# A work list that knows VectorE's and GpSimd's common port, v summed by VectorE alone, one-hots of build on TensorE

## The chip, the cores and the metric

The kernel runs on one core of one Trainium2 chip. TensorE (PE) multiplies matrices and loads weights (PEld), VectorE (DVE), ScalarE (ACT) and GpSimd (POOL) work element by element, SyncE (SP) issues plain DMAs, and GpSimd also issues the indirect DMAs that gather rows by index. The metric is the time of one execution in microseconds (us); lower is better. Of the kernel before there are three timed runs: 3367.77, 3373.03 and 3373.15 us, median 3373.03.

## The reference

Two transformer blocks follow each other on one sequence of 256 tokens of width 2048, in float32. The change lies in the last part, the PEER layer (product keys, `peer_sublayer`) of the second block. For each of two blocks of 128 tokens, 8 heads and 16 choices a head:

```
q = (hb @ w_query).reshape(PEER_BLOCK, PEER_HEADS, 2, D_KEY // 2)
s = jnp.einsum('thpc,hpnc->thpn', q, sub_keys).astype(jnp.float32)
top_s, top_i = lax.top_k(s, PEER_TOPK)
cand_s = (top_s[:, :, 0, :, None] + top_s[:, :, 1, None, :]).reshape(PEER_BLOCK, PEER_HEADS, -1)
cand_i = (top_i[:, :, 0, :, None] * N_KEYS + top_i[:, :, 1, None, :]).reshape(PEER_BLOCK, PEER_HEADS, -1)
best_s, best_j = lax.top_k(cand_s, PEER_TOPK)
idx = jnp.take_along_axis(cand_i, best_j, axis=-1)
g = jax.nn.softmax(best_s, axis=-1)
u_sel = jnp.take(u, idx, axis=0)
a = jax.nn.gelu(jnp.einsum('thkd,td->thk', u_sel, hb), approximate=False)
v_sel = jnp.take(v, idx, axis=0)
return jnp.einsum('thk,thkd->td', (g * a).astype(hb.dtype), v_sel)
```

`u` and `v` have 16384 rows (128 x 128 pairs of half keys) of 2048 columns each. A token picks 8 x 16 = 128 experts, so both blocks together have 256 gathers of 128 rows, one row for each token of a block.

## The kernel before

Everything up to the PEER layer is scheduled by the framework. The PEER layer is ordered by `Plan`, a list of operations with their estimated costs, run once while the program is built: each engine has a clock, an operation is ready when what it comes after is done, and the engine that can start first takes the ready operation with the lowest key. `plan.choice` offers an operation to two engines, and the clocks choose. The order that comes out is the order of each engine's instructions; on the chip nothing of the costs is left, only waits for data and for buffers. A `ring` stands for the buffers of one tile.

The stages, in the order of time:

- **Query and routing** (`plan_query`, `plan_route`): 32 tiles of `w_query` are split into a high and a low part (`hi` on ACT, `lo` on DVE or POOL), multiplied with the tokens, and 16 units (head and block) pick their 16 best keys on DVE. POOL multiplies the one-hot places `eq` with the keys' numbers (L1568).
- **Scores** (`plan_scores`, `plan_gather_u`): the upper 1024 columns of all u rows are multiplied densely on PE in 128 tiles e, into S. The lower 1024 columns are gathered for the chosen rows only, and multiplied with the tokens by DVE (L1680) or by POOL and ACT (L1686, L1687).
- **Pick** (`plan_pick`): the chosen scores are taken out of S. For 4 tokens at once PE forms a distance between key numbers from their digits (`far`, L1789), ACT makes a one-hot matrix of it with Relu (`near`, L1793), PE multiplies (L1798), DVE selects (L1804). `plan_coef` then makes the weights `cf` of a block: gelu times softmax.
- **Build** (`plan_weights`): S is filled again, now with the weights of all 16384 experts for each token. For 4 tokens DVE makes two one-hot matrices by comparing an iota with the key numbers, `ohb` (L1858) and `oha` (L1864, four instructions, times the weight), PE multiplies them (L1870), ACT moves the product to S (L1874). Block 0 of build overlaps block 1 of pick.
- **Out** (`plan_out`, `plan_gather_v`): columns 768 to 2047 of v are multiplied densely on PE in 128 tiles e: load `vraw`, `vhi` on ACT (L1953), `vlo` on DVE (L1957), the weights' halves `wh` on ACT and `wl` on DVE (L1965), and three products (hi hi, lo hi, hi lo) in that order (L1970). Columns 0 to 767 are gathered for the chosen rows (L1902) and summed: DVE multiplies and adds in one instruction into `vacc0` (L1909), or ACT scales (L1916) and POOL adds into `vacc1` (L1921); at the end the two are merged (L2007).

An indirect DMA stands in POOL's own instruction stream, so POOL's sums and the gathers queue behind each other. SP issues all loads in order.

## Time and profile before

| what | value |
|---|---|
| median of three runs | 3373.03 us |
| profiled execution | 3370.8 us, span 3369.1 us |
| PE busy, share of span | 2915.7 us, 87% |
| VectorE busy | 2602.2 us, 77% |
| GpSimd busy | 1492.3 us, 44% |
| DMA, mean over the span | 224 GB/s |

The span runs from the first to the last instruction; 1.7 us lie around it. The PEER layer's own stages begin at about 1754 us. A window's row gives each engine's busy time in it, then the granted clock of TensorE (1.0 is 2.4 GHz, 0.5 is 1.2 GHz), the DMA engines' busy share, and GB/s. Busy time of an instruction includes time in which it has been started and is held up.

### The profile page before, as it was taken

How to read it: one execution, taken by the hardware profiler on the slowest of the kernel's cores; microseconds unless marked ns; L12 is line 12 of the kernel's file. 1: busy time of each engine (PE TensorE's matmuls, PEld its weight loads, DVE VectorE, ACT ScalarE, POOL GpSimd, SP SyncE). 2: the span in 40 equal slices, each digit the busy share in tenths (PEclk: the TensorE clock that was granted, in tenths of full speed). 3: DMA queues.
4: the chain of work that ended last, by engine and by line, in shares of the span. 5: the costliest groups of instructions: out<-in, count | busy, mean ns of one | idle time of the engine just before them, and what ended most of it. 6: DMA issues, size and time to landing. Idle time of an engine off the chain costs nothing.

```text
span 3369.1 us, 45653 instructions
## 1 busy us (share of the span) xinstructions
PE 2915.7 (87%) x16134; PEld 2456.3 (73%) x16134; DVE 2602.2 (77%) x4256; ACT 1646.7 (49%) x2629; POOL 1492.3 (44%) x994
## 2 busy tenths in 40 slices
PE   3598899799999999999988889998977767888887
PEld 1475677677888778988768788888865655777775
DVE  7879877868656655555558998888867998999898
ACT  5555545545444544544544444444434455555554
POOL 3324433402000000000005666788867757988887
PEclk9699998899999999999989899999977878999999
DMA  8777876756655555544565378999965337888887
GB/s 298 231 253 250 280 244 216 257 164 221 181 157 162 175 157 144 151 132 137 156 223 185 118 225 299 342 340 338 348 201 174 112 89 246 288 308 292 303 297 248
DMA packets 293393, 753.05 MB, mean 224 GB/s; under 512 B 32430, under 2 KB 39524, under 8 KB 292780
## 3 DMA queue, kind: packets, MB, share of 16 engines
q1 hardware_dynamic: 235216, 513.03, 48.0%
q0 software_dynamic: 57344, 234.91, 20.0%
q8 instruction: 127, 2.08, 0.3%
q10 hardware_dynamic: 604, 2.19, 0.2%
q14 instruction: 102, 0.84, 0.1%
HBM read 743.48 MB, written 6.55 MB: 223 GB/s over the span
## 4 chain that ended last, share of the span: by engine, by line
PE 38%; DVE 20%; DMA 12%; POOL 12%; issue 10%; ACT 3%; POOLq 0%; DVEq 0%; SPq 0%; ACTq 0%
PE b_mm L387 7%; PE b_mm L386 7%; PE b_mm L388 7%; DMA mraw<-in_w_mod 6%; PE b_mm L1970 4%; DMA gathered<-in_peer_u,idx 3%; POOL gathered L1686 3%; POOL vacc L1921 3%; POOL gathered L1674 3%; DVE vlo L1957 2%; POOL gathered L1902 2%; PE b_mm L408 2%; PE b_mm L406 2%; PE b_mm L407 2%; DVE lo L361 2%
## 5 line engine op out<-in xcount | busy, mean ns | idle before, releaser
L361 DVE TENSOR_TENSOR lo<-raw,hi 128x1024 fp32r<-128x1024 f32 (+2 forms) x456 | 571.6, 1255 | 351.9 <-ACT hi L360 349.9
L360 ACT CAST hi<-raw 128x1024 fp32r<-128x1024 f32 (+2 forms) x456 | 464.6, 1021 | 453.6 <-PE b_mm L388 275.9
L387 PE MATMUL b_mm<-lo,hh 128*128 128x512 f32 (+1 forms) x1536 | 620.0, 404 | 30.0 <-DVE lo L361 26.8
L388 PE MATMUL b_mm<-hi,hl 128*128 128x512 f32 (+1 forms) x1536 | 604.3, 398 | 0.5 <-DVE hl L638 0.5
L386 PE MATMUL b_mm<-hi,hh 128*128 128x512 f32 (+1 forms) x1536 | 581.7, 402 | 9.3 <-ACT hi L360 7.1
L1902 POOL DMA_INDIRECT gathered<-in_peer_v,idx x256 | 333.7, 1303 | 99.6 <-issue 31.2
L387 PEld LDWEIGHTS b_mm<-lo,hh 128*128 128x128 f32 x1536 | 295.3, 192 | 109.7 <-DVE lo L361 49.6
L1674 POOL DMA_INDIRECT gathered<-in_peer_u,idx x256 | 296.0, 1156 | 163.0 <-DVE gathered L1680 53.9
L554 POOL TENSOR_TENSOR macc<-macc,mraw 128x512 f32<-128x512 f32 x112 | 179.6, 1604 | 420.8 <-ACT mraw L552 386.0
L386 PEld LDWEIGHTS b_mm<-hi,hh 128*128 128x128 f32 x1536 | 293.3, 192 | 84.2 <-ACT hi L360 11.5
L388 PEld LDWEIGHTS b_mm<-hi,hl 128*128 128x128 f32 x1536 | 293.9, 192 | 62.7 <-DVE hl L638 1.0
L1680 DVE SCALAR_TENSOR_TENSOR gathered<-gathered,hn 128x1024 f32<-128x1024 f32 x159 | 284.3, 1802 | 65.7 <-DMA gathered<-in_peer_u,idx 65.5
L1741 PE MATMUL b_mm<-hd,ulo 128*128 128x256 f32 x1024 | 301.8, 295 | 27.3 <-DVE ulo L1731 26.5
L1739 PE MATMUL b_mm<-hd,uhi 128*128 128x256 f32 x1024 | 308.6, 301 | 10.4 <-ACT uhi L1727 10.0
L1921 POOL TENSOR_TENSOR vacc<-vacc,gathered 128x768 f32<-128x768 f32 x154 | 302.0, 1961 | 33.4 <-ACT gathered L1916 30.4
L1740 PE MATMUL b_mm<-hd,uhi 128*128 128x256 f32 x1024 | 294.2, 287 | 0.0
L1957 DVE TENSOR_TENSOR vlo<-vraw,vhi 128x1280 fp32r<-128x1280 f32 x128 | 268.2, 2096 | 3.9 <-ACT vhi L1953 3.7
L1686 POOL TENSOR_TENSOR gathered<-gathered,hn 128x1024 f32<-128x1024 f32 x97 | 235.7, 2430 | 24.5 <-DMA gathered<-in_peer_u,idx 19.7
L1741 PEld LDWEIGHTS b_mm<-hd,ulo 128*128 128x128 f32 x1024 | 200.5, 196 | 40.9 <-DVE ulo L1731 40.5
L1970 PE MATMUL b_mm<-vlo,wh 128*128 128x512 f32 x512 | 166.2, 417 | 65.7 <-DVE vlo L1957 65.6
L1739 PEld LDWEIGHTS b_mm<-hd,uhi 128*128 128x128 f32 x1024 | 201.0, 196 | 14.4 <-ACT uhi L1727 14.3
L1740 PEld LDWEIGHTS b_mm<-hd,uhi 128*128 128x128 f32 x1024 | 201.2, 196 | 0.0
(616 smaller groups left out, 6493.5 us busy)
## 6 DMA issues: line engine op xcount, KB each, us to landing
raw<-in_w_in SPq DMA_DIRECT2D x336, 512.0 KB
mraw<-in_w_mod SPq DMA_DIRECT2D x192, 512.0 KB
vraw<-in_peer_v SPq DMA_DIRECT2D x128, 640.0 KB
uraw<-in_peer_u SPq DMA_DIRECT2D x123, 512.0 KB
raw<-in_w_out SPq DMA_DIRECT2D x96, 512.0 KB
raw<-in_peer_w_query SPq DMA_DIRECT2D x32, 512.0 KB
raw<-in_w_in SPq DMA_DIRECT2D x16, 256.0 KB
gathered<-in_peer_u,idx POOLq DMA_INDIRECT x256, 7.2
```

Source lines behind the costliest of these rows:

```text
L360: nc.scalar.copy(hi[:, :, :n], raw[:, :, :n])
L361: nc.vector.tensor_tensor(lo[:, :, :n], raw[:, :, :n], hi.bitcast(F32)[:, :, :n], ALU.subtract)
L386: nc.tensor.matmul(o, ah[:, kk, s], hi[:, k, :n], start=kk == 0, stop=False)
L387: nc.tensor.matmul(o, ah[:, kk, s], lo[:, k, :n], start=False, stop=False)
L388: nc.tensor.matmul(o, al[:, kk, s], hi[:, k, :n], start=False, stop=kk == KT - 1)
L1674: nc.gpsimd.indirect_dma_start(out=g, out_offset=None, in_=rows, in_offset=bass.IndirectOffsetOnAxis(ap=self.idx[h, t][:, k:k + 1], axis=0))
L1686: nc.gpsimd.tensor_tensor(s["g"], s["g"], self.hn[:, t, :], ALU.mult)
L1739: nc.tensor.matmul(o, h["hi"][:, k, :], hh[:, kk, :], start=kk == 0, stop=False)
L1740: nc.tensor.matmul(o, h["hi"][:, k, :], hl[:, kk, :], start=False, stop=False)
L1741: nc.tensor.matmul(o, h["lo"][:, k, :], hh[:, kk, :], start=False, stop=kk == UD - 1)
L1902: nc.gpsimd.indirect_dma_start(out=g, out_offset=None, in_=rows, in_offset=bass.IndirectOffsetOnAxis(ap=self.idx[h, t][:, k:k + 1], axis=0))
L1921: plan.op("POOL", 2.05, lambda o: nc.gpsimd.tensor_tensor(a, a, s["g"], ALU.add), key - 12, after=[o], frees=[(gv, s["op"]), (poolq, o)], ...
```

## The change

- `Plan` gets a clock `shared`. An operation that is marked (`two`, or `True` behind its cost) starts in the list only when the previous marked one is over, on whichever engine. Marked are DVE operations of several kinds and POOL's product of gathered u rows. Several costs are new numbers.
- The low halves of `w_query` (1024 columns) that stood on POOL, 11 of the 32, and the 16 products of `eq` with the keys' numbers (512 columns) go from POOL to DVE.
- Every sum of gathered v rows is done by DVE into one `vacc`; ACT's scaling, POOL's adding, `vacc1` and the merge are gone.
- `GV` goes from 768 to 736, so PE's dense part of v is 1312 columns wide. There are 4 gather buffers of v at first, not 3. In the list, gathers from number 90 on come after the load of a tile e that rises with the number ("tied to tiles"). On the chip this is no wait: it sets places in the engines' order.
- Build's one-hots come from digits, as pick's do: PE forms distances for both key numbers (`far`: 8 matmuls of 128 columns on 32 rows), DVE compares the one in PSUM with zero distance and multiplies with the weight in a single instruction (`ohb`), and ACT makes the other with Relu (`oha`). For this the digits of both key numbers are split, stored and loaded again; squares and casts of them go to ACT. Pick's and build's distances use the `mm` banks, build's products the `tr` banks.

```diff
-GV = 768
+GV = 736
+RX = 4
+EARLY = 90
...
     def start(self, o, a):
-        t = max(self.clock[a[0]], o.ready)
+        t = max(self.clock[a[0]], o.ready, self.shared if a[5] else 0.0)
...
             end = self.clock[e] = t + cost
+            if two:
+                self.shared = end
...
-                c = plan.choice([("DVE", 1.28, lambda o, f=lo: f(o, nc.vector), (), 0),
-                                 ("POOL", 2.5, lambda o, f=lo: f(o, nc.gpsimd), (), 0)], key - 80, after=[b],
-                                takes=[r[2]], frees=[(r[0], a)])
+                c = plan.op("DVE", 1.26, lo, key - 80, after=[b], takes=[r[2]], frees=[(r[0], a)], two=True)
...
-        def marked(o):
+        def negated(o):
             nm = s["nm"] = sp.tile([P, 1], F32, name="nm", tag="nm", bufs=2)
             nc.gpsimd.tensor_scalar(nm, s["best"][:, 0:1], -1.0, None, op0=ALU.mult)
-            nc.gpsimd.tensor_tensor(s["eq"], s["eq"], s["indf"][:, :, None, :].to_broadcast(FOUR), ALU.mult)
...
         def numbers(o):
+            nc.vector.tensor_tensor(s["eq"], s["eq"], s["indf"][:, :, None, :].to_broadcast(FOUR), ALU.mult)
...
-                plan.choice([("DVE", 1.42, dot, (), 0), ("POOL", 2.5, product, (poolq,), 0)], key, after=[o])
+                plan.choice([("DVE", 1.31, dot, (), 0, True), ("POOL", 2.45, product, (poolq,), 0, True)], key,
+                            after=[o])
...
+            def far(o, n=n, s=s):
+                r1, r, c = self.distance(t, n)
+                s["p1"], s["p2"] = self.bank("mm", 4), self.bank("mm", 4)
+                for i in range(4):
+                    nc.tensor.matmul(s["p1"][:, i * P:(i + 1) * P], r1[:, i * P:(i + 1) * P], c, start=True, stop=True)
+                for i in range(4):
+                    nc.tensor.matmul(s["p2"][:, i * P:(i + 1) * P], r[:, i * P:(i + 1) * P], c, start=True, stop=True)
+
+            def first(o, n=n, s=s):
                 s["b"] = self.vp.tile([P, 4, P], F32, name="ohb", tag="ohb", bufs=3)
-                nc.vector.tensor_tensor(s["b"], self.iota[:, None, :].to_broadcast([P, 4, P]),
-                                        self.byexp[t][:, 1, n:n + 4, None].to_broadcast([P, 4, P]), ALU.is_equal)
-
-            def first(o, n=n, s=s):
-                s["a"] = a = self.vp.tile([P, 4, P], F32, name="oha", tag="oha", bufs=4)
+                nc.vector.scalar_tensor_tensor(s["b"], s["p1"].rearrange("p (a b) -> p a b", a=4), 1.0,
+                                               self.byexp[t][:, 2, n:n + 4, None].to_broadcast([P, 4, P]),
+                                               op0=ALU.is_equal, op1=ALU.mult)
+
+            def second(o, s=s):
+                s["a"] = self.vp.tile([P, 4, P], F32, name="oha", tag="oha", bufs=3)
+                nc.scalar.activation(s["a"], s["p2"].rearrange("p (a b) -> p a b", a=4), AF.Relu)
...
-                        nc.scalar.activation(a if fresh else s["g"], s["g"], AF.Identity, scale=c)
...
-                            plan.op("POOL", 2.05, lambda o: nc.gpsimd.tensor_tensor(a, a, s["g"], ALU.add), key - 12,
...
+                    o = plan.op("POOL", 1.08, gather, key - 25, after=[*last, *pace], takes=[gv], kb=GV / 2)
                     last = [o.issued]
-                    plan.choice([("DVE", 1.06, add, (), 0), ("ACT", 0.98, scale, (poolq,), 0)], key,
-                                after=[o, self.cf_done[t][1]])
+                    plan.op("DVE", 0.12 + GV * 1.16e-3, add, key, after=[o, self.cf_done[t][1]], frees=[(gv, o)],
+                            signals=[self.added], two=True)
```

Where the list places things, at three places. **VectorE in build**, where blocks 1 of pick (`pjunk`) and 0 of build meet. Before:

```order
L1804 SCALAR_TENSOR_TENSOR pjunk,dots_22902<-iota_22905,byexp_22904,b_at 128x128 x4
L1858 TENSOR_TENSOR ohb<-iota_22905,byexp_22903 128x512
L1864 TENSOR_SCALAR oha<-iota_22905,byexp_22903 128x128 x4
L1858 TENSOR_TENSOR ohb<-iota_22905,byexp_22903 128x512
L1804 SCALAR_TENSOR_TENSOR pjunk,dots_22902<-iota_22905,byexp_22904,b_at 128x128 x4
L1864 TENSOR_SCALAR oha<-iota_22905,byexp_22903 128x128 x4
```

Now, at the same place:

```order
L1932 SCALAR_TENSOR_TENSOR vacc<-gathered,cf_23638,vacc 128x736
L1815 SCALAR_TENSOR_TENSOR pjunk,dots_22905<-iota_22908,byexp_22907,b_at 128x128 x4
L1877 SCALAR_TENSOR_TENSOR ohb<-b_mm,byexp_22906 128x512
L1932 SCALAR_TENSOR_TENSOR vacc<-gathered,cf_23638,vacc 128x736 x2
L1815 SCALAR_TENSOR_TENSOR pjunk,dots_22905<-iota_22908,byexp_22907,b_at 128x128 x4
L1877 SCALAR_TENSOR_TENSOR ohb<-b_mm,byexp_22906 128x512
```

The five comparisons of a tile on VectorE have become one, and sums of gathered v rows (L1932) stand between. In the order before, 7 sums stand on VectorE ahead of the first `wl` of out; now 83 do, 26 of them ahead of block 1's weights.

**VectorE in out**, in the middle of the tiles. Before:

```order
L1965 TENSOR_TENSOR wl<-S,wh 128x256
L1909 SCALAR_TENSOR_TENSOR vacc_22892<-gathered,cf_24598,vacc_22892 128x768
L1957 TENSOR_TENSOR vlo<-vraw,vhi 128x1280
L1965 TENSOR_TENSOR wl<-S,wh 128x256
L1957 TENSOR_TENSOR vlo<-vraw,vhi 128x1280
```

Now:

```order
L1975 TENSOR_TENSOR wl<-S,wh 128x256
L1932 SCALAR_TENSOR_TENSOR vacc<-gathered,cf_24776,vacc 128x736
L1967 TENSOR_TENSOR vlo<-vraw,vhi 128x1312
L1932 SCALAR_TENSOR_TENSOR vacc<-gathered,cf_24776,vacc 128x736
L1975 TENSOR_TENSOR wl<-S,wh 128x256
L1967 TENSOR_TENSOR vlo<-vraw,vhi 128x1312
```

A tile has one or two sums on VectorE; 88 of the 256 stand ahead of the first `vlo`, 179 ahead of the 65th, and the last one stands ahead of the 123rd.

**GpSimd in out.** Before:

```order
L1902 DMA gathered<-in_peer_v,idx 128x768 x2
L1921 TENSOR_TENSOR vacc_22893<-vacc_22893,gathered 128x768
L1902 DMA gathered<-in_peer_v,idx 128x768 x2
L1921 TENSOR_TENSOR vacc_22893<-vacc_22893,gathered 128x768
L1902 DMA gathered<-in_peer_v,idx 128x768
```

Now, from the last product of u rows to the end:

```order
L1684 DMA gathered<-in_peer_u,idx 128x1024 x3
L1696 TENSOR_TENSOR gathered<-gathered,hn 128x1024
L1925 DMA gathered<-in_peer_v,idx 128x736 x252
L2050 UNCONDITIONAL_BRANCH
```

No sum is left on GpSimd behind the u rows. Of the 256 gathers of u, 214 stood ahead of pick's first instruction on GpSimd (an iota) and 42 behind it; now 208 and 48.

## Rows read from the trace of the kernel before

**Rows 1.** Busy time by stage: routing and scores, scores' end alone, pick, pick/build, build, out.

```profile
1754.00:2457.00 703.00, 622.75 (x4938) 600.52 (x4936) 596.82 (x1084) 310.77 (x583) 495.27 (x338) 0.97 0.78 271
2076.00:2457.00 381.00, 346.01 (x2742) 330.09 (x2741) 316.83 (x396) 167.44 (x311) 307.92 (x208) 0.98 0.93 337
2457.00:2567.00 110.00, 82.71 (x318) 61.53 (x319) 70.21 (x325) 36.85 (x66) 73.53 (x53) 0.72 0.59 190
2567.00:2704.00 137.00, 100.84 (x463) 83.92 (x461) 131.02 (x390) 65.55 (x88) 103.55 (x72) 0.79 0.45 136
2704.00:2813.00 109.00, 56.84 (x313) 51.71 (x313) 101.34 (x198) 56.93 (x65) 64.29 (x44) 0.72 0.35 105
2813.00:3358.00 545.00, 479.17 (x2304) 389.79 (x2304) 501.75 (x349) 297.54 (x360) 481.10 (x301) 0.97 0.86 294
```

**Rows 2.** Waits in out, 2813 to 3358: total, times, longest.

```profile
PE b_mm L1970 <- DVE vlo L1957: 65.6, 64, 2.8
```

**Rows 3.** Groups by line in out, 2813 to 3358: busy, mean ns, idle before.

```profile
L1957 DVE TENSOR_TENSOR vlo<-vraw,vhi 128x1280 fp32r<-128x1280 f32 x128 | 268.2, 2096 | 3.9 <-ACT vhi L1953 3.7
L1902 POOL DMA_INDIRECT gathered<-in_peer_v,idx x194 | 267.3, 1378 | 55.1 <-issue 27.0 <-POOL vacc L1921 17.9 <-DVE vacc L1909 7.9
...
L1909 DVE SCALAR_TENSOR_TENSOR vacc<-gathered,cf,vacc 128x768 f32<-128x768 f32 x91 | 141.5, 1555 | 26.7 <-DMA gathered<-in_peer_v,idx 26.5
L1965 DVE TENSOR_TENSOR wl<-S,wh 128x256 fp32r<-128x256 f32 x126 | 110.4, 876 | 10.9 <-PE b_at L1970 7.0 <-ACT gathered L1916 1.2 <-ACT wh L1961 0.2
```

**Rows 4.** Single lines of VectorE: durations min/median/max in ns, first and last start.

```profile
L1957 DVE TENSOR_TENSOR vlo<-vraw,vhi x128: 1476/1479/3830, 2814.0 to 3352.3; 128x1280 fp32r<-128x1280 f32 x128
L1909 DVE SCALAR_TENSOR_TENSOR vacc<-gathered,cf,vacc x100: 1002/1045/3295, 2667.2 to 3342.0; 128x768 f32<-128x768 f32 x100
L1965 DVE TENSOR_TENSOR wl<-S,wh x128: 408/412/2806, 2802.6 to 3351.9; 128x256 fp32r<-128x256 f32 x128
```

**Rows 5.** Instructions in order of time in out: start, us, engine, line.

```profile
3002.83 3.80 DVE L1957 TENSOR_TENSOR vlo<-vraw,vhi 128x1280 fp32r<-128x1280 f32 x1
...
3003.43 1.85 POOL L1921 TENSOR_TENSOR vacc<-vacc,gathered 128x768 f32<-128x768 f32 x1
...
3003.78 0.30 PEld L1970 LDWEIGHTS b_mm<-vhi,wl 128*128 128x128 f32 x2
...
3004.95 0.31 PEld L1970 LDWEIGHTS b_mm<-vhi,wh 128*128 128x128 f32 x2
...
3005.44 2.04 POOL L1902 DMA_INDIRECT gathered<-in_peer_v,idx  x1 [0.17 <-issue]
...
3007.78 0.95 POOL L1902 DMA_INDIRECT gathered<-in_peer_v,idx  x1 [0.30 <-issue]
3007.82 1.48 DVE L1957 TENSOR_TENSOR vlo<-vraw,vhi 128x1280 fp32r<-128x1280 f32 x1
```

**Rows 6.** Groups by line in build, 2567 to 2813.

```profile
L1864 DVE TENSOR_SCALAR oha<-iota,byexp 128x128 f32<-128x128 f32 x256 | 134.8, 588 | 0.0
L1870 PE MATMUL b_mm<-oha,ohb 128*128 128x128 f32 x512 | 94.3, 350 | 51.4 <-DVE ohb L1858 35.0 <-DVE oha L1864 12.4 <-ACT S L1874 3.4
...
L1798 PE MATMUL b_at<-S,ohf 128*128 128x128 f32 x236 | 58.6, 406 | 19.4 <-DVE pjunk L1804 17.5 <-ACT gathered L1916 1.8
L1858 DVE TENSOR_TENSOR ohb<-iota,byexp 128x512 f32<-128x512 f32 x64 | 50.4, 792 | 0.0
...
L1804 DVE SCALAR_TENSOR_TENSOR pjunk<-iota,byexp,b_at 128x128 f32<-128x128 f32 x120 | 33.9, 335 | 1.6 <-PE b_at L1798 1.6
...
L1789 PE MATMUL b_tr<-rows,digits 32*128 32x512 bf16 x25 | 10.3, 419 | 4.7 <-ACT ohf L1793 3.6 <-ACT byexp L1838 1.0
```

**Rows 7.** Groups by line in pick, 2457 to 2567.

```profile
L1674 POOL DMA_INDIRECT gathered<-in_peer_u,idx x37 | 42.9, 1160 | 26.8 <-DVE gathered L1680 17.9 <-DVE pjunk L1804 3.7 <-issue 3.4
```

**Rows 8.** Groups by line in routing and scores, 1754 to 2457.

```profile
L1741 PE MATMUL b_mm<-hd,ulo 128*128 128x256 f32 x1024 | 301.8, 295 | 27.3 <-DVE ulo L1731 26.5
...
L1731 DVE TENSOR_TENSOR ulo<-b_tr,uhi 128x512 fp32r<-128x512 f32 x144 | 97.4, 682 | 24.8 <-ACT uhi L1727 24.5
```

More of the change, by code (lines that the diff above doesn't have):

```diff
@@ L167, in __init__, with op @@
         self.transfers = 0.0
+        self.shared = 0.0
         self.left = 0
         self.now = 0.0
-    def op(self, engine, cost, fn, key, after=(), takes=(), frees=(), signals=(), kb=0):
-        return self.choice([(engine, cost, fn, (), kb)], key, after, takes, frees, signals)
+    def op(self, engine, cost, fn, key, after=(), takes=(), frees=(), signals=(), kb=0, two=False):
+        return self.choice([(engine, cost, fn, (), kb, two)], key, after, takes, frees, signals)
     def choice(self, alts, key, after=(), takes=(), frees=(), signals=()):
@@ L233, in run @@
             assert best is not None, "nothing can go on"
-            t, _, _, o, (e, cost, fn, takes, kb) = best
+            t, _, _, o, (e, cost, fn, takes, kb, two) = best
             for a in o.alts:
@@ L1361, in peer @@
         self.added = Event(2 * PH * TOPK)
-        self.rowed = Event(2)
+        self.rowed = [Event(2) for _ in range(2)]
         units = self.plan_query()
@@ L1375, in peer @@
         chosen = plan.op("ctl", 0, self.open_pick, 0, after=[late, self.left_ud, self.scored])
+        for p, _, back in digits[2:]:
+            plan.op("SP", 0.4, back, 600, after=[chosen], kb=128, signals=[self.rowed[p]])
         keyno = [self.plan_keyno(t, chosen) for t in range(2)]
@@ L1412, in open_pick @@
         self.va = self.pool(self.st, "va")
-        self.vacc = [self.va.tile([P, 2, GV], F32, name="vacc%d" % i) for i in range(2)]
-        nc.sync.dma_start(self.vacc[0], self.x_kept[:, :, :GV])
-        self.fresh = [True, True]
+        self.vacc = self.va.tile([P, 2, GV], F32, name="vacc")
+        nc.sync.dma_start(self.vacc, self.x_kept[:, :, :GV])
         self.rx = self.pool(self.st, "rx")
-        self.gv.add([(self.rx, "x%d" % i) for i in range(3)], self.plan.now)
+        self.gv.add([(self.rx, "x%d" % i) for i in range(RX)], self.plan.now)
         self.vs = ExitStack()
@@ L1424, in open_pick @@
         nc.sync.dma_start(spread, self.C["spread"])
+        self.rows[0] = self.lp.tile([P, 8 * P], BF16, name="rows0")
         self.digits = self.lp.tile([P, 8, P], BF16, name="digits")
@@ L1876, in move @@
                     s["ps"].rearrange("p (t e) -> p t e", t=4))
-            mm, ra, rb = ring("mm", 4), ring("oha", 4), ring("ohb", 3)
-            a = plan.op("DVE", 0.64, second, key - 6, after=[coef[2]], takes=[rb])
-            b = plan.op("DVE", 0.9, first, key - 4, after=[coef[2]], takes=[ra])
-            c = plan.op("PE", 1.6, products, key, after=[a, b], takes=[mm], frees=[(rb, a), (ra, b)])
-            plan.op("ACT", 1.05, lambda o, f=move: f(o, nc.scalar), key, after=[c], frees=[(mm, c)],
+            tr, mm, ra, rb = ring("tr", 2), ring("mm", 4), ring("oha", 3), ring("ohb", 3)
+            f = plan.op("PE", 0.46, far, key - 6, after=[self.far, *self.rowed, coef[1]], takes=[mm, mm])
+            b = plan.op("DVE", 0.7, first, key - 5, after=[f, coef[2]], takes=[rb], frees=[(mm, f)])
+            a = plan.op("ACT", 0.62, second, key - 5, after=[f], takes=[ra], frees=[(mm, f)])
+            c = plan.op("PE", 1.5, products, key, after=[a, b], takes=[tr], frees=[(ra, a), (rb, b)])
+            plan.op("ACT", 1.05, lambda o, f=move: f(o, nc.scalar), key, after=[c], frees=[(tr, c)],
                     signals=[self.weighed])
@@ L1890, in plan_gather_v @@
         n, last = 0, [chosen]
-        poolq = self.ring("poolv", 2)
+        self.paced = [[] for _ in range(P)]
         for t in range(2):
```

117 lines of the change are left out of this document (54 added, 63 removed).

## The prediction

> **What bounds the kernel now.** I read the busy times by stage first, then the waits in the last stage, then its groups by line and the single instructions behind their means. Everything up to 1754 us lies ahead of the PEER layer, where no engine's order changes, so it stands at 1754 us on both sides. Behind it the stages are long by very different reasons [rows 1]. Routing and scores (703 us) are PE's: 623 us busy at a clock of 0.97. In pick (110 us) no engine is full: VectorE 70, PE 83. In pick with build (137 us) VectorE is full with 131, in build (109 us) with 101, and PE runs at a granted clock of 0.79 and 0.72. Out, 545 us and the largest of the four, has VectorE at 502, PE at 479 and GpSimd at 481.
>
> The wait that ends last in out is PE's for `vlo`, 65.6 us in 64 waits [rows 2]. The reader is to see why `vlo` is late: its median is 1.479 us, its mean 2.096 [rows 3, 4]. The mean hides two cases. At 3007.82 it takes 1.48 us; at 3002.83 it takes 3.80, and in that time POOL's sum runs from 3003.43 to 3005.28; 3.80 less what is left after 3005.28 is the wait, since 3005.28 + 1.48 is close to its end at 3006.63 [rows 5]. So VectorE doesn't run slower beside POOL: it is held until POOL's sum is over. Over out this costs 128 x (2.096 - 1.479) = 79 us for `vlo`, 91 x (1.555 - 1.02) = 49 for the sums and 126 x (0.876 - 0.412) = 58 for `wl`, 186 of VectorE's 502 us [rows 1, 3, 4]. 1.02 lies between the minimum and the median of the sums.
>
> Not all POOL work does this. The gather at 3007.78 runs its 0.95 us while `vlo`, begun 0.04 us later, still takes 1.48 [rows 5]. The other way round a gather is held: that of 3005.44 takes 2.04 us, and ends 0.85 us after the `vlo` in front of it.
>
> **The change part by part.** The sum is made against the profiled execution's 3370.8 us (span 3369.1 and 1.7 around it). It lies 2.2 us under the median, inside the 5.4 us that the three runs spread, so the result is read as a median unchanged. A measurement of this kernel tells about 0.2% (7 us) from nothing.
>
> Out. PE's floor: the loads of the sets (hi, wl) and (hi, wh), 1.17 us apart, are back to back [rows 5], so a tile of three sets takes 3.51 us at 1280 columns and 3.60 at 1312; 128 tiles take 461 us. Another floor is PE's busy time, 479 us, which holds the ends that are drawn out before each wait [rows 1]: times 1312/1280 that is 491. VectorE: 128 `vlo` at 1.479 x 1312/1280 = 1.516 make 194, 128 `wl` at 0.412 make 53, and the 168 sums that stand behind the first `vlo` at 1.02 x 736/768 = 0.98 make 165: 412 us, under PE's 461 and no longer held, since POOL has no sum left. DMA: before, 294 GB/s x 545 us = 160 MB; now 128 loads of 672 KB and about 164 gathers of 377 KB, 148 MB, which is 311 GB/s over 476 us. The engines were 0.86 busy at 294, so 0.91 [rows 1]. I take 476 us, the lower floor and 15 us for tiles with two sums and for late landings: -69. Bounds: -84 at the floor, -20 if a good half of the waits for `vlo` stays on the longer floor (491 + 34).
>
> Where the adds are late they hold VectorE in order, and `vlo`, then PE, behind them. Seven buffers turn over once in 7/1.31 tiles, 19 us; a gather is issued in at most 2.04 + 0.30 us [rows 5], and its landing has the rest. In SP's order the store of `vacc` stands ahead of the last two loads of v, and waits for all 256 sums; the last sum stands ahead of the 123rd `vlo`, whose end frees the buffer of the 127th load, so this costs nothing; if that cover went, one load's time, under 10 us. The merge goes: -1.
>
> Pick with build, 137 us. VectorE now has 120 selections (34 us [rows 6]), 10 u products of 1024 columns (at 1.36, twice the 0.68 that `ulo` takes for 512 [rows 8], 14 us), 24 `ohb`, and 26 sums at 0.98 = 25. `ohb` of the new kind isn't in the trace: it reads one operand in PSUM, 512 columns, as `ulo` does in 0.682; the row of the old `ohb` gives 0.792 [rows 6]. I take 0.68, 16 us: 89 in all, against 131. Then PE is late next: 30 pick tiles of 8 x 58.6/236 = 1.99 us and a distance of 0.42 are 72 us; 24 build products of 94.3/64 = 1.47 are 35; and 24 times the new distance. Of that, 8 short matmuls on 32 rows, no row shows the price: at least two of the old ones (0.84, twice the columns), at most 8 of the old ones (3.4) [rows 6]; being a quarter as wide each, I take 0.8: 19. PE has 126, so -11. Bounds: -30 (VectorE's 89 and the chain of waits in between) and +10.
>
> Build, 109 us to the first product of out. VectorE: 40 x 0.68 and 61 sums at 0.98 = 87. POOL: some 55 gathers at 1.378 and 0.3 between [rows 3, 5] = 92. PE: 40 x (1.47 + 0.8) = 91. ACT loses the scaling and gains Relu, and was 57 of 109 [rows 1]. With three engines near 90 and 8 us until the first tile of v is there, 98: -11. Bounds: -22 and +17 (PE at the lower clock, or the gathers as in the third rival).
>
> Pick, 110 us. It is paced by the u gathers: 37 in 110 us, one in 3.0, through three buffers [rows 7]; six more are left over than before, at most 18 us. But block 0 needs only the first 16 of the 48, and what stands ahead of its weights is four more u products on VectorE, 4 x 1.36: +5. Bounds 0 and +18.
>
> Routing and scores, 703 us. VectorE gets 11 halves of 1024 columns at 1.36, 16 products at 0.68 and two more splits, some 5 us: 31 us, part of it beside PE's scores. PE waits for `ulo` 26.5 us in this stage [rows 8], part of which is VectorE held behind POOL; that goes with 11 halves and 16 products less on POOL. The six gathers that wait longer for their buffers are priced in pick. I take -5, bounds -26 and +25.
>
> Sum: -69 - 1 - 11 - 11 + 5 - 5 = -92, so 3370.8 - 92 = 3279 us.
>
> **A rule against this change.** The row shows one gather held to 2.04 us and one at 0.95 [rows 5]. The Trainium skill, SBUF — State Buffer, section "SBUF: two separate sides", warns that an indirect DMA's descriptors can't be written while VectorE holds the port pair, which fits the first row; its section "Who interferes with whom" infers that a `tensor_tensor` leaves descriptor writing alone, which the first row contradicts, as `vlo` is one. By the warning, taken for every gather, the result is the third rival's; by the inference it is the forecast's.
>
> **The rivals.** First, DMA bounds out. For: VectorE waited 26.5 us for gathers in out at 294 GB/s [rows 1, 3]. 148 MB at 294 are 503 us, so out gives 42, not 69: 3306. Against: at the end of scores, also loads and gathers together, 337 GB/s were moved at 0.93 [rows 1].
>
> Second, on the other side: it isn't POOL's sums that hold VectorE but any GpSimd instruction, gathers included, and VectorE alone with all sums is the bound. At the means of the rows a tile costs 2.096 x 1.025 + 0.876 + 1.31 x 1.555 x 0.958 = 4.98 us [rows 3], 637 in all: +92 instead of -69, so 3440. The total is slower from VectorE at 1.38 times its floor of 412 us (568 us, where the other terms' gain of 23 is eaten up); before it stood at 1.56 (520 us for 334). For it: 194 gathers run in out, 267 us of them. Against: the pair at 3007.78.
>
> Third, the gathers starve: VectorE is busier now, and each gather waits for it: 2.34 us. In build 55 take 129 us, +20 instead of -11; in out 168 take 393, hidden under 476: 3310.
>
> Fourth, the change doesn't do what it says: what was waited for at `vlo` is waited for elsewhere in VectorE's order (a late gather, `vhi`), in out and in build alike, and the three terms there come to nothing: 3370. For it: `vhi` and `vlo` have two buffers each, so a late one is felt at once. Against: VectorE's sum of work falls in both.
>
> **How the numbers follow.** Forecast 0.66, DMA 0.12, second 0.05, third 0.13, fourth 0.04. The forecast's own range is 3235 to 3325, from the bounds, the larger terms not all at one end. The range 3232 to 3330 holds it but for its ends, and the first and third rival, and leaves out the second and fourth. Faster: 0.66 + 0.12 + 0.13 and nothing of the others, 0.91; same 0.04; slower 0.05.
>
> **What would show it.** Out: `vlo` mean at 1.52 and the sums at 0.98 with no long ones, PE's wait for `vlo` under 20 us, 128 tiles in 476 us, PE's clock at 0.98 or more. Build: `ohb` at 0.68, VectorE no longer full, 85 to 100 us for the last 40 tiles. Pick 5 us longer, routing and scores within 25 us of 703. It would be wrong if `vlo` still had long cases beside gathers, if the sums' idle time for landings grew past 50 us, or if the new distances on PE took over 2 us a tile.

## The result, and the profile after

The changed kernel takes 3262.2 us (median of four executions, 3254.4 to 3265.3), the kernel before 3370.4 on the same chip (3362.7 to 3373.2): 0.968 of its time, 95% interval 0.966 to 0.970. Forecast were 3279 us, range 3232 to 3330. The profiled execution has a span of 3260.3 us. The times here are medians of executions; of the five of e8_filler, one (3267 us, at a mean granted clock of 0.932 where its others have 0.947 to 0.951) is left out of its figures.

Stage lengths in us, from marks in each trace (the first `hi` of the query, the last score moved into S, the weights `byexp` of block 0 and of block 1, the first and the last product of out):

| stage | before | after | difference | forecast |
|---|---|---|---|---|
| routing and scores | 704 | 732 | +28 | -5 |
| pick | 115 | 119 | +4 | +5 |
| pick with build | 133 | 100 | -33 | -11 |
| build, to the first product of out | 108 | 79 | -29 | -11 |
| out | 545 | 469 | -76 | -69 |
| merge and the rest | 11 | 11 | 0 | -1 |

The query begins 2 us earlier in the trace of after; with that the rows sum to -108. The same windows as in [rows 1], of the kernel after (routing and scores, scores' end alone, pick, pick with build, build, out):

```profile
1751.00:2482.00 731.00, 621.54 (x4939) 601.03 (x4939) 594.77 (x1124) 304.09 (x577) 422.76 (x298) 0.95 0.75 258
2076.00:2482.00 406.00, 361.37 (x2850) 346.76 (x2849) 315.45 (x447) 162.31 (x309) 281.84 (x200) 0.97 0.89 317
2482.00:2601.00 119.00, 84.82 (x334) 64.09 (x332) 74.69 (x336) 35.42 (x63) 70.03 (x53) 0.70 0.59 193
2601.00:2701.00 100.00, 97.92 (x658) 79.91 (x658) 86.69 (x310) 56.42 (x89) 58.64 (x46) 0.98 0.57 170
2701.00:2780.00 79.00, 64.42 (x616) 55.04 (x616) 74.45 (x96) 61.25 (x83) 61.12 (x56) 0.95 0.85 273
2780.00:3249.00 469.00, 460.79 (x2304) 394.09 (x2304) 391.44 (x429) 215.58 (x253) 225.03 (x167) 0.98 0.92 322
```

In out, VectorE went from 502 busy us to 391 and PE is busy in 461 of 469. In build the surprise is the granted clock, third from the right: 0.95, where it was 0.72.

Out's groups by line after (busy us, mean ns, idle before), which answer to [rows 3]:

```profile
L1925 POOL DMA_INDIRECT gathered<-in_peer_v,idx x167 | 225.0, 1347 | 201.5 <-DVE vacc L1932 197.0 <-DVE vlo L1967 3.0 <-issue 1.5
L1967 DVE TENSOR_TENSOR vlo<-vraw,vhi 128x1312 fp32r<-128x1312 f32 x128 | 195.1, 1524 | 46.6 <-ACT vhi L1963 46.6
L1932 DVE SCALAR_TENSOR_TENSOR vacc<-gathered,cf,vacc 128x736 f32<-128x736 f32 x173 | 169.4, 979 | 4.8 <-DMA gathered<-in_peer_v,idx 4.6
```

and VectorE's lines singly (min/median/max in ns), which answer to [rows 4]:

```profile
L1967 DVE TENSOR_TENSOR vlo<-vraw,vhi x128: 1515/1526/1551, 2789.2 to 3243.3; 128x1312 fp32r<-128x1312 f32 x128
L1932 DVE SCALAR_TENSOR_TENSOR vacc<-gathered,cf,vacc x256: 970/979/1024, 2640.4 to 3223.4; 128x736 f32<-128x736 f32 x128
L1975 DVE TENSOR_TENSOR wl<-S,wh x128: 414/419/466, 2779.0 to 3242.1; 128x256 fp32r<-128x256 f32 x128
```

The long cases are gone: the slowest of 128 `vlo` takes 1.551 us, where [rows 4] have 3.830, though 167 gathers run beside them. PE waits for `vlo` once, 8.2 us ([rows 2] have 64 times):

```profile
PE b_mm L1980 <- DVE vlo L1967: 8.2, 1, 8.2
```

From pick with build to build's end, the groups that answer to [rows 6]:

```profile
L1888 PE MATMUL b_tr<-ohb,oha 128*128 128x128 f32 x512 | 73.7, 288 | 5.4 <-DVE ohb L1877 5.1
...
L1877 DVE SCALAR_TENSOR_TENSOR ohb<-b_mm,byexp 128x512 f32<-128x512 f32 x64 | 43.8, 684 | 0.3 <-PE b_mm L1871 0.2
...
L1871 PE MATMUL b_mm<-digits,rows 32*128 32x128 bf16 x256 | 25.1, 217 | 0.0
```

A build product takes 288 ns where it took 350, `ohb` the estimated 0.68 us, and a tile's two distances 50/64 = 0.78 us (25.1 us for L1871, and 24.5 for L1873), close to the estimated 0.8.

### The profile page after: what moved, and what is told of

The parts are those of the page before. It is cut to its first block, busy times and chain, and to the rows that moved or that the text cites. A ratio compares the mean times of both kernels' runs of the same rounds, so it can differ in the third digit from the quotient of the medians.

```text
span 3260.3 us, 46369 instructions
## 1 busy us (share of the span) xinstructions
PE 2897.5 (89%) x16646; PEld 2461.6 (76%) x16646; DVE 2422.6 (74%) x4207; ACT 1550.9 (48%) x2529; POOL 1113.1 (34%) x805
## 4 chain that ended last, share of the span: by engine, by line
PE 53%; DVE 15%; DMA 12%; issue 6%; POOL 6%; ACT 3%; SPq 0%; DVEq 0%; POOLq 0%; ACTq 0%
PE b_mm L1980 11%; PE b_mm L393 7%; PE b_mm L394 7%; PE b_mm L392 7%; DMA mraw<-in_w_mod 6%; DMA gathered<-in_peer_u,idx 5%; PE b_at L1980 3%; DVE gathered L1690 2%; PE b_mm L414 2%; PE b_mm L412 2%; POOL gathered L1684 2%; PE b_mm L413 2%; DVE lo L367 2%; POOL gathered L1696 2%; PE b_at L1809 2%
## 5 line engine op out<-in xcount | busy, mean ns | idle before, releaser
L1925 POOL DMA_INDIRECT gathered<-in_peer_v,idx x256 | 324.8, 1269 | 251.8 <-DVE vacc L1932 226.6
L1752 PE MATMUL b_mm<-hd,ulo 128*128 128x256 f32 x1024 | 301.3, 294 | 28.9 <-DVE ulo L1742 28.7
L1690 DVE SCALAR_TENSOR_TENSOR gathered<-gathered,hn 128x1024 f32<-128x1024 f32 x167 | 255.9, 1551 | 77.7 <-DMA gathered<-in_peer_u,idx 76.7
L1932 DVE SCALAR_TENSOR_TENSOR vacc<-gathered,cf,vacc 128x736 f32<-128x736 f32 x256 | 250.7, 979 | 9.4 <-DMA gathered<-in_peer_v,idx 8.4
L1967 DVE TENSOR_TENSOR vlo<-vraw,vhi 128x1312 fp32r<-128x1312 f32 x128 | 195.1, 1524 | 46.6 <-ACT vhi L1963 46.6
L1696 POOL TENSOR_TENSOR gathered<-gathered,hn 128x1024 f32<-128x1024 f32 x89 | 213.6, 2400 | 20.4 <-DMA gathered<-in_peer_u,idx 18.9
L1963 ACT CAST vhi<-vraw 128x1312 fp32r<-128x1312 f32 x128 | 165.7, 1294 | 107.3 <-PE b_at L1980 99.3
```

Of the source, the lines that this page charges most:

```text
L1690: nc.vector.scalar_tensor_tensor(s["g"], s["g"], 1.0, self.hn[:, t, :], op0=ALU.mult, op1=ALU.mult, accum_out=a)
L1752: nc.tensor.matmul(o, h["lo"][:, k, :], hh[:, kk, :], start=False, stop=kk == UD - 1)
L1925: nc.gpsimd.indirect_dma_start(out=g, out_offset=None, in_=rows, in_offset=bass.IndirectOffsetOnAxis(ap=self.idx[h, t][:, k:k + 1], axis=0))
```

## The experiments

Each is the kernel after with the edit shown, unless another is named as its base. The stage lengths, in the same marks (routing is up to the last list of indices, scores from there). Each was timed with the kernel before beside it (medians 3367 to 3371 us); the number in brackets is its share of that time, with the 95% interval. Two kernels whose intervals overlap are not told apart by their totals.

| kernel | median us | routing | scores | pick | pick+build | build | out | clock in build |
|---|---|---|---|---|---|---|---|---|
| before | 3370 | 294 | 410 | 115 | 133 | 108 | 545 | 0.72 |
| after | 3262 | 317 | 415 | 119 | 100 | 79 | 469 | 0.95 |
| e1_route_pool | 3263 | 298 | 396 | 119 | 98 | 120 | 465 | 0.55 |
| e2_no_shared | 3253 | 308 | 383 | 126 | 96 | 119 | 460 | 0.57 |
| e3_v_pool | 3309 | 318 | 408 | 120 | 117 | 117 | 466 | 0.54 |
| e4_onehot_dve | 3310 | 320 | 414 | 120 | 93 | 78 | 518 | 0.90 |
| e5_untied | 3301 | 320 | 414 | 116 | 103 | 78 | 507 | 0.95 |
| e6_gv768 | 3250 | 323 | 413 | 116 | 103 | 72 | 467 | 1.00 |
| e8_filler | 3215 | 310 | 383 | 126 | 98 | 80 | 460 | 0.96 |
| e9_u_dve | 3216 | 317 | 373 | 123 | 97 | 77 | 458 | 0.95 |
| e10_u_dve_768 | 3206 | 319 | 374 | 124 | 97 | 72 | 453 | 0.99 |
| e11_stall | 3254 | 316 | 376 | 123 | 97 | 116 | 460 | 0.58 |
| e13_u_dve_route | 3201 | 311 | 369 | 124 | 97 | 78 | 460 | 0.95 |
| e14_best | 3189 | 311 | 367 | 125 | 98 | 72 | 453 | 0.99 |

**e1_route_pool: why is routing with scores longer?**

```diff
-                c = plan.op("DVE", 1.26, lo, key - 80, after=[b], takes=[r[2]], frees=[(r[0], a)], two=True)
+                c = plan.choice([("DVE", 1.26, lambda o, f=lo: f(o, nc.vector), (), 0, True),
+                                 ("POOL", 2.5, lambda o, f=lo: f(o, nc.gpsimd), (), 0, True)], key - 80, after=[b],
...
+            nc.gpsimd.tensor_tensor(s["eq"], s["eq"], s["indf"][:, :, None, :].to_broadcast(FOUR), ALU.mult)
...
-            nc.vector.tensor_tensor(s["eq"], s["eq"], s["indf"][:, :, None, :].to_broadcast(FOUR), ALU.mult)
...
```

> The changed kernel with its routing part undone: 13 halves of the low parts of the queries (lo) and the products of the 16 lists of numbers (eq) are on GpSimd again, as before; everything behind the scores keeps the change. Query to the end of the scores took 704 us before and 732 us changed. Theory 1, the 28 us are the work moved to VectorE (11 halves and 16 products, 31 us by the prediction's own rows): this stage falls to 705 to 715 us, the total from 3262 to 3235 to 3247, and VectorE's late numbers (idx of unit 16 at 2067.9 us changed, 2047.0 before) come at 2045 to 2052. Rival, they come from elsewhere (four splits of digits, other order of the u gathers): the stage stays within 5 us of 732 and the total within 5 of 3262. Rival on the other side, GpSimd's halves hold VectorE in this stage too: the stage grows to 740 us and over, the total to 3270.

The stage falls to 695 us, more than theory 1 asked for: 19 of 23 us of routing come back, and 18 in the scores beside. So the halves and lists on VectorE lengthened routing: VectorE is busy there for 256 us before, 275 after and 248 here. Why the scores gain too was not followed. Yet the total stays at 3263 (0.967, 0.965 to 0.969, of before), since build took 120 us instead of 79, with no edit there.

**e2_no_shared: is it the order that the shared clock makes?**

```diff
-        t = max(self.clock[a[0]], o.ready, self.shared if a[5] else 0.0)
+        t = max(self.clock[a[0]], o.ready)
```

> The changed kernel whose list of clocks takes no account of the shared port (one condition in the planner), so that only the order and the engine of 64 u products differ: GpSimd takes 64 of them and VectorE 192. Theory, the order that the shared clock makes is what delays the scores: query to the end of scores falls from 732 to 705 to 718 us and the total to 3237 to 3250. Rival, the order matters nothing there: 732 us within 5, total 3262 within 6. Rival on the other side, the shared clock earns its place by keeping VectorE from being held: with it gone, GpSimd's 64 products (1.9 us each) hold VectorE, the stage grows by 10 to 40 us and the total to 3272 to 3300.

The stage takes 691 us, below the range of the theory; the rival on the other side (VectorE held more often) is refuted. The clock that was to keep VectorE free had sent more u products to GpSimd, 89 against 64, and 40 against 15 of them into the scores. The total is 3253 (0.964, 0.963 to 0.966), although build again took 119 us. So the shared clock, the first part of the change, costs 41 us in routing and scores instead of earning its place.

**What happened in build.** The window of build in e2:

```profile
2663.50:2783.00 119.50, 107.75 (x616) 92.81 (x616) 74.76 (x93) 65.87 (x84) 65.24 (x54) 0.57 0.64 188
```

Compared with the row 2701 to 2780 of after, above, VectorE has the same work (74.76 and 74.45 us), but PE is busy for 107.75 us instead of 64.42, at a clock of 0.57 instead of 0.95. PE in e1, in order of time, where the same happens (start, us, engine, line, idle before):

```profile
2673.00 1.16 PE L1890 MATMUL b_tr<-ohb,oha 128*128 128x128 f32 x8
2674.09 0.39 PE L1873 MATMUL b_mm<-digits,rows 32*128 32x128 bf16 x4
2675.95 0.38 PE L1875 MATMUL b_mm<-digits,rows 32*128 32x128 bf16 x4 [1.46 <-issue]
2676.26 2.06 PE L1890 MATMUL b_tr<-ohb,oha 128*128 128x128 f32 x8
```

PE stood still for 1.46 us in which nothing that the profile shows held it; the eight products behind that take 2.06 us, those before it took 1.16. A second stop of 1.48 us follows 3 us later. From 2676 us on to the last build tile, 102 us, the granted clock is the lower level (1.2 GHz). At that level a tile's products take PE 2.06 us and its distances some 1.2 (43.6 us for 37 tiles), and PE is the bound; at the upper one VectorE is, until PE waits for v.

**e8_filler, on e2: denser products for PE in build.**

```diff
+                if t == 1:
+                    nc.tensor.matmul(s["p1"][:, :], self.rows[1][:, :P], self.rows[1][:, :512], start=True, stop=True)
```

> The run without the shared clock (3253 us) with one matrix product more in each of the 32 build tiles of block 1: 512 columns of bf16 against a full 128x128 stationary, into a bank that the tile's distance overwrites next; its result is not used. In the run without it, PE ran build at a granted clock of 0.57 with hardly a gap (108 of 120 us busy), in the changed kernel at 0.95 (64 of 79 us). Theory, build is as long as the clock makes it, and denser products lift the clock: the clock of build comes to over 0.85, build from 120 to 80 to 95 us, the total to 3213 to 3230. Rival, the clock stays at the lower level whatever PE does there, and the filler only adds 0.43 us a tile: build 130 to 138 us, total 3263 to 3272. Rival 2, build isn't long because of PE at all (VectorE, gathers): build within 4 of 120.

```profile
2670.00:2750.00 80.00, 70.86 (x649) 55.88 (x650) 71.93 (x94) 61.05 (x83) 59.73 (x54) 0.96 0.84 266
```

PE is busy for 71 us here and for 64 in after; build takes 80 us instead of 119, and the total is 3215 (0.954, 0.951 to 0.956). In this trace PE had no gap over 0.3 us until the last build tile, where e2 had one of 1.9. So the run shows that build is short when the clock stays up, not whether the filler would lift a clock that had fallen, nor whether it is the filler that kept it up.

**e9_u_dve: no product on GpSimd at all.**

```diff
-                plan.choice([("DVE", 1.31, dot, (), 0, True), ("POOL", 2.45, product, (poolq,), 0, True)], key,
-                            after=[o])
+                plan.op("DVE", 1.2, dot, key, after=[o], two=True)
```

> The changed kernel with all 256 u products on VectorE as well (167 before, 89 on GpSimd with ACT), so that GpSimd has no product or sum left behind the query. Theory, GpSimd's u products hold VectorE just as its v sums did: an undisturbed u product takes VectorE 1.22 us, its mean in the scores was 1.67. Routing: 35 products more (43 us) less the 47 us that VectorE was held: 312 us of 317. Scores: 54 more (66 us) less 122 x 0.45 = 55, but PE's waits for ulo (37 us) go: 375 to 390 of 414. Query to the end of scores 685 to 705 instead of 732. Build is 79 us where the clock stays at full and 120 where it falls, so the total is 3215 to 3240 or 3255 to 3275. Rival, VectorE is the bound of routing and scores and the added work counts in full: 732 + 40 to 60 us, total 3300 to 3320.

VectorE's u products in the scores, 2066 us to their end, of after and then of this kernel:

```profile
L1690 DVE SCALAR_TENSOR_TENSOR gathered<-gathered,hn 128x1024 f32<-128x1024 f32 x122 | 201.3, 1672 | 53.0 <-DMA gathered<-in_peer_u,idx 52.5 <-issue 0.5
```

```profile
L1690 DVE SCALAR_TENSOR_TENSOR gathered<-gathered,hn 128x1024 f32<-128x1024 f32 x178 | 214.2, 1220 | 21.8 <-DMA gathered<-in_peer_u,idx 21.1
```

178 products take 13 us more than 122 did, since none is held: the longest takes 1.27 us here and 3.80 in after. Scores fall from 415 to 373 us, routing stays at 317, and the clock of build holds: 3216 (0.954, 0.953 to 0.956). The rival, that the added work counts in full, is refuted.

**e11_stall, on e9: one wait of PE, put in.** The first one-hot of block 1 is written seven times over.

```diff
-                nc.vector.scalar_tensor_tensor(s["b"], s["p1"].rearrange("p (a b) -> p a b", a=4), 1.0,
+                for _ in range(7 if (t, n) == (1, 0) else 1):
+                  nc.vector.scalar_tensor_tensor(s["b"], s["p1"].rearrange("p (a b) -> p a b", a=4), 1.0,
```

> The run with all u products on VectorE (3216 us), in which the one-hot of the first build tile of block 1 is written seven times over by VectorE with the same result: 6 x 0.69 = 4.1 us more once, for which PE has to wait some 3 us. Theory, build is long where PE stood still for 1.5 us or more shortly before, because the granted clock then falls and doesn't come back until out: clock of build 0.55 to 0.65, build from 78 to 115 to 125 us, the total to 3250 to 3262, ten times what the stall itself takes. Rival, a single wait doesn't hold the clock down: build 78 to 84 us, the total 3216 to 3222.

The place in the trace, and build without and with the wait (e9's window, then e11's):

```profile
2684.12 5.04 DVE L1877 SCALAR_TENSOR_TENSOR ohb<-b_mm,byexp 128x512 f32<-128x512 f32 x7
...
2689.21 2.08 PE L1888 MATMUL b_tr<-ohb,oha 128*128 128x128 f32 x8 [4.23 <-DVE ohb L1877]
```

```profile
2659.00:2736.60 77.60, 64.57 (x617) 55.20 (x617) 69.81 (x92) 61.38 (x84) 55.19 (x52) 0.95 0.86 276
```

```profile
2672.00:2788.00 116.00, 104.25 (x617) 90.00 (x618) 76.48 (x98) 65.03 (x84) 61.85 (x52) 0.58 0.65 191
```

A wait of 4.2 us costs 38 in the total, 3254 against 3216 (0.965, 0.964 to 0.966, of before): the clock falls at 2687 us, 2 us into the wait, and stays down until the last build tile. This is the theory's number; the rival is refuted. Of the runs it is the one that changes nothing but the wait.

**e3_v_pool: sums of v on GpSimd again.** Two accumulators, ACT scales and GpSimd adds, by choice; three buffers for raw tiles instead of four.

```diff
...
-                    plan.op("DVE", 0.12 + GV * 1.16e-3, add, key, after=[o, self.cf_done[t][1]], frees=[(gv, o)],
-                            signals=[self.added], two=True)
+                    plan.choice([("DVE", 0.12 + GV * 1.16e-3, add, (), 0, True), ("ACT", 0.98, scale, (poolq,), 0, False)],
+                                key, after=[o, self.cf_done[t][1]])
...
```

> The changed kernel with the sums of v shared again: VectorE takes 191 of them, ACT with GpSimd 65, in two accumulators with a merge; three buffers for the raw tiles instead of four, for lack of space. Theory, GpSimd's sums hold VectorE as they did before: the low parts of v (vlo, 1.526 us each changed) are 1.8 to 2.1 us in the mean, with cases over 3 us, the last stage grows from 469 to 500 to 540 us, the total to 3295 to 3335. Rival, the last stage became shorter because PE no longer has to wait for anything but is bound by its own products, and the order alone did that: vlo stays under 1.6 us or its long cases cost PE nothing, the total stays within 10 us of 3262.

The total, 3309 (0.982, 0.980 to 0.984), falls in the theory's range, but not for its reason: out is 466 us, not 500 and more. `vlo`, VectorE's groups by line and out in this kernel:

```profile
L1982 DVE TENSOR_TENSOR vlo<-vraw,vhi x128: 1509/1526/3280, 2829.9 to 3289.9; 128x1312 fp32r<-128x1312 f32 x128
```

```profile
L1982 DVE TENSOR_TENSOR vlo<-vraw,vhi 128x1312 fp32r<-128x1312 f32 x128 | 214.3, 1675 | 26.8 <-ACT vhi L1978 26.0 <-issue 0.8
L1934 DVE SCALAR_TENSOR_TENSOR vacc<-gathered,cf,vacc 128x736 f32<-128x736 f32 x137 | 141.6, 1033 | 5.4 <-DMA gathered<-in_peer_v,idx 5.3
L1990 DVE TENSOR_TENSOR wl<-S,wh 128x256 fp32r<-128x256 f32 x126 | 73.2, 581 | 25.1 <-PE b_at L1995 20.4 <-ACT wh L1986 2.2 <-ACT gathered L1941 0.9
```

```profile
2830.00:3296.00 466.00, 462.62 (x2304) 389.81 (x2304) 408.51 (x396) 238.83 (x282) 291.63 (x191) 1.00 0.89 320
```

The long cases are back (3.280 us), but with 28 sums on GpSimd in out, where before had 107, VectorE is at 409 of 466 us and what it is held for is hidden under PE. The 47 us were lost ahead of it: 17 in pick with build, and 38 in build, at a clock of 0.54. Against after's means the 28 sums hold VectorE for 128 x 0.151 + 137 x 0.054 + 126 x 0.160 = 47 us, 1.7 us each; in before 107 held it for 186, also 1.7 each. So an estimate from these rows for 107 sums is some 180 us, where VectorE has 57 us free here. That they would bring out back to 545 was not run.

**e4_onehot_dve: build compares on VectorE again.**

```diff
...
-            f = plan.op("PE", 0.46, far, key - 6, after=[self.far, *self.rowed, coef[1]], takes=[mm, mm])
-            b = plan.op("DVE", 0.7, first, key - 5, after=[f, coef[2]], takes=[rb], frees=[(mm, f)])
-            a = plan.op("ACT", 0.62, second, key - 5, after=[f], takes=[ra], frees=[(mm, f)])
...
+            a = plan.op("DVE", 0.64, second, key - 6, after=[coef[2]], takes=[rb], two=True)
+            b = plan.op("DVE", 1.33, first, key - 4, after=[coef[2]], takes=[ra], two=True)
...
```

> The changed kernel whose build compares on VectorE again (one-hots from iota, two kinds, 2.1 us a tile), with two splits of digits instead of four; the rest keeps the change. Theory, VectorE bounds pick with build and build (179 us together changed): 64 tiles x (2.1 - 0.69) = 90 us more on VectorE, which fall to that stretch but for the sums of v that move behind it (16 instead of 85 before the first vlo, 69 x 0.98 = 68 us), so the stretch grows by 25 to 50 us and the last stage, where VectorE has 78 us free of 469, by 0 to 15: total 3290 to 3320. Rival, PE's new products cost as much as they save: the stretch stays within 10 us of 179 and the total within 10 of 3262. If the two further splits of digits are what delays the scores (732 us against 704 before), that stage falls by 10 to 20 us here, otherwise it stays within 5.

3310 us (0.982, 0.980 to 0.984) lies in the theory's range, with the places wrong: the stretch of pick with build and build is 171 us, 8 shorter than after, and out 49 longer. The old one-hots of both kinds are no longer slow once GpSimd has no sums:

```profile
L1874 DVE TENSOR_SCALAR oha<-iota,byexp 128x128 f32<-128x128 f32 x256 | 72.5, 350 | 0.0
L1868 DVE TENSOR_TENSOR ohb<-iota,byexp 128x512 f32<-128x512 f32 x64 | 44.1, 688 | 0.0
```

against 588 and 792 ns in [rows 6]: 256 x 0.238 + 64 x 0.104 = 68 us of before's build were VectorE being held. What the new one-hots give is room for some 70 sums of v ahead of out; without it out has 243 where after has 173, PE waits 30 us for `vlo`, and out takes 518 us. The splits of digits do not delay the scores (734 us).

**e5_untied: gathers of v tied to no tile.**

```diff
-EARLY = 90
+EARLY = 256
```

> The changed kernel with the gathers of v tied to no tile (EARLY 256 instead of 90). GpSimd's and PE's order stay the same; on VectorE the 168 sums that stand behind the first vlo are done by tile 90 of out instead of tile 123. Theory, the tie matters a little: in those 90 tiles VectorE has 1.87 sums x 0.98 + 1.53 + 0.42 = 3.78 us a tile, over PE's 3.60, so out grows by up to 90 x 0.18 = 16 us, and the gathers ask for more of the DMA's time next to the loads: 469 becomes 475 to 490, the total 3268 to 3283. Rival, PE stays ahead through its buffers and nothing changes: out 469 within 4, total within 6 of 3262.

3301 us (0.978, 0.976 to 0.981): the tie is worth 39 us, more than the theory's upper end. The same stretch of out here, and below it in after:

```profile
2833.00:2933.00 100.00, 92.22 (x451) 75.75 (x450) 91.45 (x100) 41.37 (x51) 72.71 (x51) 1.00 0.97 360
```

```profile
2830.00:2930.00 100.00, 100.00 (x507) 85.69 (x506) 87.47 (x97) 47.61 (x56) 57.12 (x41) 1.00 0.97 345
```

25 tiles in 100 us (451 products of 18 a tile) against 28. VectorE is at 91 with one, two or four sums between two `vlo`, and waits for PE itself at every second `wl` (36 of 74, 26 us in 300); that wait in its order, 0.35 us a tile, is what the theory's 3.78 us a tile left out, against 4.03 in the trace.

**e6_gv768, and e10_u_dve_768 on e9: the gathered part of v wider.**

```diff
-GV = 736
+GV = 768
```

> The changed kernel with the gathered part of v back at 768 columns (736 changed), so 1280 instead of 1312 in the loaded part. Theory, PE bounds out now (461 of 469 us busy changed): a tile of three sets goes from 3.60 to 3.51 us and out from 469 to 457 to 462; the sums take 1.01 us instead of 0.98, which costs VectorE 5 us of its 78 free ones there and 3 us in the two stages before; total 3250 to 3258. Rival, VectorE or the landings of the gathers are as near to the bound as PE: out stays within 4 of 469, total 3260 to 3270.

> The run with all u products on VectorE (3216 us) and 768 gathered columns of v instead of 736. Theory, PE bounds out there too: 128 tiles of 3.51 instead of 3.60 us, out from 458 to 446 to 452, the total to 3203 to 3211. Rival, with PE's floor lower the landings or VectorE end last: out within 3 of 458, total 3212 to 3222.

3250 (0.965, 0.963 to 0.967) and 3206 (0.952, 0.950 to 0.953): 12 and 10 us less, the totals as forecast, though e6's interval overlaps after's. The places are not. In the traces PE's step from tile to tile falls from 3.57 to 3.52 us, half of the 0.09 forecast. Out gives 2 us (467 against 469, within the rival's 4) and 5 (453 against 458 on e9). Build gives 7 and 5, where the first load of v is issued 4 us ahead of the end of build's last product and not behind it.

**e13_u_dve_route, on e9: halves and lists on GpSimd, the edit of e1; e14_best with the wider part as well.** e13 is e1's edit on e9; e14 adds:

```diff
-GV = 736
+GV = 768
```

> The run with all u products on VectorE (3216 us), with 15 halves of the queries' low parts and the 16 products of the lists of numbers on GpSimd again. Theory, VectorE bounds routing (it takes 317 us there), and what leaves it shortens routing: 15 x 1.25 + 16 x 0.58 = 28 us less, but the GpSimd pieces (15 x 2.4 + 16 x 1.2 = 55 us) hold VectorE for a part of their time, so 8 to 20 us remain: routing 297 to 309, total 3196 to 3210 if the clock of build holds, 40 more if it falls. Rival, what GpSimd's pieces hold VectorE for is as much as they take off it: routing within 5 of 317, total within 6 of 3216 (or 40 more).

> The run with all u products on VectorE and the queries' halves and lists on GpSimd again (3201 us), with 768 gathered columns of v. Theory, what each gave alone adds up: 768 columns gave 10 us with all u products on VectorE (3216 to 3206), so 3191, range 3184 to 3198, if the clock of build holds; 40 us more where it falls. Rival, the wider gathers cost in routing and build what out gains: 3197 to 3205.

3201 (0.950, 0.948 to 0.951) and 3189 us (0.947, 0.946 to 0.949): routing gives 6 us, less than the 8 to 20 expected, scores 4, and e14 the sum that was forecast. The same edit gave 19 us of routing in e1, so routing's length isn't VectorE's work alone: VectorE is busy there for 255 of 311 us in e13. e14 is faster than the kernel after by 73 us.

## Why the prediction was right, and where not

**Out** (-69, measured -76): right by its steps. VectorE's 412 us came to 391, no `vlo` is long, and PE sets the pace, at 3.57 us a tile (3.60 forecast). The 15 us above the floor were put down to tiles with two sums and to late landings; after, they are 12, and 8.2 of them are PE's one wait for the first `vlo`. Of the 76 us, e4, with all sums on VectorE but the old one-hots, has 27; the other 49 hang on the 70 sums that the new one-hots let VectorE do ahead of out. Gathers are still held, at 1347 ns in the mean against 0.95 us for the one in [rows 5], and wait 197 us for their buffers, but VectorE waits only 4.6 us for them. The inference of the Trainium skill that the prediction weighed (SBUF — State Buffer, section "Who interferes with whom"), that a `tensor_tensor` leaves descriptor writing alone, is not borne out by such gathers. No run separates the writing of descriptors from the reading of `idx`, and for the time it makes no difference. The bound by DMA (first rival) is not met: 322 GB/s at 0.92. e4 and e5 show how near VectorE's own bound is: 70 sums more, or the same ones unevenly, lengthen out by 38 to 49 us.

**Build, and pick with build** (-11 each, measured -29 and -33): right in sign, the terms mis-sized. PE's 91 us for 40 tiles were worked out at 1.47 us a product, a duration of a stretch that ran at 0.72 to 0.79 of the clock; at 0.95 they are 1.16, and PE is busy for 64 us. POOL's 92 us used the gathers of out, 1.378 us; here they took 1.10. So none of the three engines stood near 90: VectorE is busy in 74 of the 79 us, and the last 9.4 are PE's wait for the first tile of v. These two stages are short without the new one-hots too: e4, with the old ones, no sum on GpSimd and 13 sums on VectorE instead of 83, has 171 us for them, after 179, before 241. In pick with build PE's rows were summed to 126 us; after, the same rows sum to 112 and PE is busy for 98, since they overlap. The bound of +17 for "PE at the lower clock" was a real case: e1, e2, e3 and e11 have it, at 116 to 120 us. Which one it would be, the prediction couldn't tell from before; that the changed kernel is on the good side, worth some 40 us, is luck.

**Routing and scores** (-5, measured +28, outside the bound of +25): the step that failed. Routing alone lost 23 us: the 31 us that go to VectorE were taken to be partly hidden beside PE, but VectorE's busy time there rose by 19 us and routing with it, and e1, which takes them off, gives 19 back (e13, on e9, only 6). In the scores the relief did not come: PE's wait for `ulo` was 28.7 us in the two stages after ([rows 8] have 26.5):

```profile
L1752 PE MATMUL b_mm<-hd,ulo 128*128 128x256 f32 x1024 | 301.3, 294 | 28.9 <-DVE ulo L1742 28.7
```

since 75 u products were still on GpSimd (82 before), 40 of them in the scores. The prediction applied its own finding, VectorE held until GpSimd's instruction is over, to v and not to u; e9 does that and gains 42 us there.

**Pick** (+5, measured +4): the number is right, the cause isn't. The four us stand at pick's start, where `digits` waits for the load of `spread`; before and after:

```profile
2465.31 1.23 DVE L1426 TENSOR_TENSOR digits<-spread 128x1024 bf16<-128x1024 f32 x1 [5.11 <-DMA spread<-const_spread]
```

```profile
2494.33 1.23 DVE L1434 TENSOR_TENSOR digits<-spread 128x1024 bf16<-128x1024 f32 x1 [13.26 <-DMA spread<-const_spread]
```

That is 8.1 and 11.8 us behind the end of the scores; from there to the weights of block 0 both kernels take 107 us, so the u products that are left over add nothing that these traces show. Why the load lands later is open.

**The sum** came within 16 us of the forecast because +33 in routing and scores met -47 in the other stages. That is luck too.

The second and the fourth rival are refuted by `vlo`'s 1.551 us at most and by the result; the third is half right: gathers are slowed, at no cost.

## What to carry to other kernels

Where an engine is held rather than slow (a mean far over the median), look at every instruction of the other engine that does it, in every stage, before the ones of the stage in front of you. Price a stretch at the clock that it will have, not at the one in the row: two terms here came out nearly three times as large as forecast, in part for that. An edit in one stage can turn the clock of another, so compare stages, not totals: e1 and after have the same total and differ by 37 and 41 us in two of them.
